# Hybrid decoder step: adaLN shifts taken out of PSUM by ScalarE, S5 tables a unit sooner, one Toeplitz tile for four quarters

## The chip, the cores and the metric

One Trainium2 chip, one NeuronCore of it. The metric is device time in microseconds of one execution; the median of three runs of the kernel before is 1148.75 us.

## The reference

One layer of a decoder works on 1024 prompt positions and 8 single-token sequences with a state of their own. An adaLN vector, `mod = silu(c) @ ada_w + ada_b`, gives shift, scale and gate for two blocks. The first block is what the change touches:

```python
hn = rmsnorm(x, norm1_g) * (1.0 + sc1) + sh1
proj = hn @ w_in                        # 1024 x 1536: RG-LRU input, its gate, S5 input u
# RG-LRU half: causal conv of width 4, gates, real recurrence, times gelu(gate)
# S5 half: 32 groups of 16 channels, each one complex diagonal state of 64
h[t] = a * h[t-1] + B u[t]              # complex, zero-order hold
y[t] = Re(C h[t]) + d * u[t];  z = gelu(y) @ w_glu;  out = za * sigmoid(zb)
```

Both halves are normalised and go through `w_out`, are gated and added to `x`; then come a SwiGLU feed-forward block and a final norm. Outputs are all tokens and the new states.

## The kernel before, in words

Activations lie as feature x token, 1032 tokens wide. Matmuls run with each float32 operand split into a high and a low part, three matmuls for one product (L142 to L144, the helper `mm3`); the split's low part is a VectorE subtraction and appears as `wl_...`.

The stage around the change is the input projection. Its twelve 128-column blocks of `w_in`, in three pieces of 344 tokens, make 36 pieces; the first six are computed in an opening. The other 30 are called units here and stand in the list `SEQ` (L1062), each of 8 x 3 matmuls into one PSUM bank. The rest of the stage is hung in front of units by `at(i, function)` (L1059). What is hung there is the remaining adaLN work (`rest_load`, `rest_dot`, `rest_out`) and the S5 half, in four quarters of eight groups each. A quarter `f_` starts at unit `STARTS[f_]`, that is 5, 9, 14 or 19, and takes these steps at offsets from it (L1055):

- `s5_in_tables`: from the load `bc` the scaled input matrices `bb` (VectorE), their copy `bst` (ScalarE), and the products `pb` (GpSimd, in quarter 0 VectorE).
- `s5_out_tables`: output products `cw` on VectorE, and `ost` from them by ScalarE in two pairs, one for the real and one for the imaginary half.
- `s5_turn`: TensorE transposes `pb` into `ppt`, ScalarE copies to `pst`.
- `s5_toeplitz`: TensorE multiplies `bst` by `ost` into `kp`, ScalarE copies it to `kt`, two VectorE rows add `d`; `kt` goes to DRAM as `kd` (four transfers), and eight transfers read it back as the Toeplitz tile `tm`, which GpSimd has filled with zero.
- `s5_drive` in two halves: TensorE forms `pv` from `u` and `pst`, ScalarE copies to `vt`. Behind the second half comes `s5_state` on VectorE: rotation `rw`, scan, rotation back `dw`; ScalarE copies it to `xt`.
- `s5_out` in two halves: TensorE adds `tm` times `u` and `ost` times `xt` into `py`, ScalarE applies GeLU.

`kp`, `pv`, `ppt`, `py` and the adaLN sums (`pmod`) share two PSUM tiles in turn, so each must wait until the reader of the one before last is done. That reader is VectorE's `mod` row (L69) behind a `pmod`, and ScalarE's `pst`, `vt`, `kt` rows behind others.

`ada_out` (L241) turns a finished adaLN product into `mod`, or, for part 0, into the shifts `shf`; the helper `ada_sum` (L236) does the matmul (`pmod`) and one VectorE row adds the bias `ada_b`. The shifts are then split into the last ten columns of `hnh` and `hnl` (L726) and multiplied with the first two blocks of `w_in` (`bias_dot`, L1064: `pa_b`; `adas_b` is its copy out of PSUM).

TensorE's order is the program's own in the whole kernel. In the opening this also holds for the other engines. In the stage of the 30 units, ScalarE, VectorE, GpSimd and the SyncE queue of transfers take an order that a scheduler made when the program was built. Each engine then runs its list in that order.

Of the kernel before, what the change touches and what calls it, by code (L numbers as in the profile page):

```python
# [9 lines left out]
F32 = mybir.dt.float32  # L10
F32R = mybir.dt.float32r
I32 = mybir.dt.int32
AF = mybir.ActivationFunctionType
# [5 lines left out]
P = 128  # L19
# [35 lines left out]
def body(ctx, tc, a, o):  # L55
    nc = tc.nc
    V, S, G, PE = nc.vector, nc.scalar, nc.gpsimd, nc.tensor
# [10 lines left out]
    def tt(out, x, y, op, e=None):  # L68
        (e or V).tensor_tensor(out=out, in0=x, in1=y, op=op)  # L69
# [16 lines left out]
    def stt(out, x, s, op0, y, op1):  # L86
        V.scalar_tensor_tensor(out=out, in0=x, scalar=s, in1=y, op0=op0, op1=op1)  # L87
# [4 lines left out]
    def small(name):  # L92
        return psm.tile([P, 512], F32, tag="sm", name=name)
# [23 lines left out]
    def par(name):  # L117
        s, w = PACK_AT[name]
        return pk[:, s:s + w]
# [84 lines left out]
    mod = cp.tile([P, 4, DK, 9], F32, name="mod")  # L204
    shf = cp.tile([P, DK, 32], F32, name="shf")
    G.memset(shf, 0.0)
    adab = par("ada_b").rearrange("p (a d) -> p a d", a=6)
# [28 lines left out]
    def ada_sum(sb, pt, n=9, step=16):  # L236
        for i in range(2):
            PE.matmul(pt[:, i * step:i * step + n], lhsT=sb[:, i * P:(i + 1) * P], rhs=sel[:, 0:n], start=True,
                      stop=True)

    def ada_out(sb, pt, part, h):  # L241

        ada_sum(sb, pt, 32, 32)
        d = slice(4 * h, 4 * h + 4)
        dst = mod[:, part - 2, d] if part else shf[:, d, 0:9]
        tt(dst.rearrange("p (q c) n -> p q c n", q=2),
           pt[:, 0:64].rearrange("p (c q n) -> p q c n", c=2, q=2)[:, :, :, 0:9],
           adab[:, part, d].rearrange("p (q c) -> p q c", q=2).unsqueeze(3).to_broadcast([P, 2, 2, 9]), ALU.add)
# [248 lines left out]
    bias = cp.tile([P, 12, 9], F32, name="bias")  # L497
# [157 lines left out]
    for i in range(1, 4):  # L655
        d = 2 * i
# [44 lines left out]
    rsb[1] = ada_second(sh_raw[1], "h1", sb)  # L701
    rstd_spread(r1, "n1", rb1, lambda i: small if i == 2 else lambda n: acc_bank(n, 512))
    ada_out(*rsb[1], 0, 0)
    rsb[2] = ada_dot(sh_raw[2], "h2", small, last=False)
    for c in range(NC):
# [51 lines left out]
    sp2 = []  # L757
    sq = [{} for _ in range(4)]
# [106 lines left out]
    def s5_toeplitz(f_):  # L865

        bst, ost = sq[f_]["bst"], sq[f_]["ost"]
        kp = small(f"kp{f_}")
        for g in range(8):
            st = g % 4  # L870
            PE.matmul(kp[32 * st:32 * st + 32, (g // 4) * P:(g // 4 + 1) * P], lhsT=bst[:, g], rhs=ost[:, g, 0:128],
                      start=True, stop=True, tile_position=(0, 32 * st))
        kt = sp2[0].tile([P, 2, P], F32, tag="kt", bufs=1, name=f"kt{f_}")
        S.activation(kt.rearrange("p a k -> p (a k)"), kp[:, 0:2 * P], AF.Copy)
        for i in range(2):
            stt(kt[:, i, 0:16], sel[:, 0:16], par("dk")[:, 2 * f_ + i:2 * f_ + i + 1], ALU.mult, kt[:, i, 0:16], ALU.add)
        kd = dr.tile([2, 4, 16, P], F32, name=f"kd{f_}")
        for st in range(4):
            nc.sync.dma_start(out=kd[:, st].rearrange("a c k -> c a k"), in_=kt[32 * st:32 * st + 16])
        tm = sp2[0].tile([P, 8, P], F32, tag="tm", bufs=1, name=f"tm{f_}")  # L880
        G.memset(tm, 0.0)
        for j in range(8):
            nc.sync.dma_start(out=tm[16 * j:16 * j + 16, :, 16 * j:],
                              in_=kd.rearrange("a s c k -> c (a s) k")[:, :, 0:P - 16 * j])
        sq[f_]["tm"] = tm
# [158 lines left out]
    def rest_out(j):  # L1044
        p, i = rest[j]
        if j % 2:
            ada_out(rsb[j][0], PB(f"pmod{j}"), p, i // 2)
            if p == 0:
                shift_cols(i - 1)
                shift_cols(i)  # L1050
# [1 line left out]

    R0, R1 = 4, 1.12
    STARTS = (5, 9, 14, 19)
    IT, OT, RT, TZ, DA, DB, OA, TN, OB = 5, 0, 1, 2, 1, 2, 3, 1, 2  # L1055
    CLOSE = 27
    before, mids = {}, {}

    def at(i, fn, *args):  # L1059
        before.setdefault(i, []).append((fn, args))  # L1060
# [19 lines left out]
    for j in range(4, 20):  # L1080
        i = int(R0 + R1 * (j - 4))
# [4 lines left out]
    for f_ in range(4):  # L1086
        i0 = STARTS[f_]
        at(max(0, i0 - IT), s5_in_tables, f_)
        at(max(0, i0 - OT), s5_out_tables, f_)
        at(max(0, i0 - RT), s5_rot, f_)  # L1090
        at(i0 if f_ == 0 else i0 - TN, s5_turn, f_)
        at(i0 + TZ, s5_toeplitz, f_)
        at(i0 + DA, s5_drive, f_, 0)
        at(i0 + DB, s5_drive, f_, 1)
        at(i0 + DB + OA, s5_out, f_, 0)
        at(i0 + DB + OA + OB, s5_out, f_, 1)
# [696 lines left out]
    for mp in range(4):  # L1793
        pool, tag = (hp, "H") if mp < 2 else (fp, "F")
# [157 lines left out]
```

## Time and profile before

| | us |
|---|---|
| runs of the kernel before | 1144.76, 1148.75, 1149.11 |
| the profiled execution | 1144.03, its span 1142.2 |
| TensorE matmul busy | 1086.4 (95%) |
| VectorE busy | 812.9 (71%) |
| ScalarE busy | 518.9 (45%) |
| GpSimd busy | 446.1 (39%) |
| granted TensorE clock, mean | 0.974 of full speed |

The profile is of one execution, and its instructions have start and duration. Busy times are averages over the whole span; between 50 and 250 us TensorE is less busy than later, and VectorE more than its average. The number in brackets behind a row is the time that its engine sat idle before it and what ended this; a wait for several things is put down to the one that came last. A group of equal rows is merged into one with a count, and the trace counts each float32 matmul of a small tile twice.

### The profile page before, as it was taken

The numbers are of one execution on the slowest core, as the hardware profiler recorded it, in microseconds if no ns is written. First come the engines' busy times: TensorE is split into PE (matmuls) and PEld (weight loads), VectorE is DVE, ScalarE is ACT, GpSimd is POOL, SyncE is SP. The second block draws the span as 40 slices with busy tenths as digits, with TensorE's granted clock in tenths as the row PEclk, the third lists the DMA queues.
The fourth block names the chain that finished last, engine by engine and source line by source line (L and its number), as shares of the span: only waits on it lengthen the run. The fifth ranks groups of instructions, "written<-read, shape, count | busy, mean of one in ns | idle before, by whom it ended". The sixth has DMA issues, their size and how long they took to land.

```text
span 1142.2 us, 21509 instructions
## 1 busy us (share of the span) xinstructions
PE 1086.4 (95%) x8508; PEld 1037.0 (91%) x8508; DVE 812.9 (71%) x1335; ACT 518.9 (45%) x979; POOL 446.1 (39%) x478
## 2 busy tenths in 40 slices
PE   8988979998898999899999999999999999999996
PEld 5877868897878999799999999999999999999995
DVE  6596899735966288887587577768645367778967
ACT  4544544439573066555455444545444522122254
POOL 2754665101100014675475466557342133242003
PEclk8989989999998999899999999999999999999998
DMA  9566446341143303153453245334313967468303
GB/s 336 216 188 219 156 146 217 85 130 37 40 148 111 112 38 112 37 205 118 143 186 148 85 177 186 109 131 180 120 56 102 358 264 283 166 238 275 115 8 142
DMA packets 90629, 174.94 MB, mean 153 GB/s; under 512 B 18720, under 2 KB 54304, under 8 KB 90528
## 3 DMA queue, kind: packets, MB, share of 16 engines
q1 hardware_dynamic: 90528, 173.57, 44.1%
q8 instruction: 67, 1.10, 0.4%
q14 instruction: 34, 0.28, 0.1%
HBM read 126.56 MB, written 46.98 MB: 152 GB/s over the span
## 4 chain that ended last, share of the span: by engine, by line
PE 79%; DVE 12%; ACT 3%; issue 3%; DMA 2%; SPq 1%; DVEq 0%; ACTq 0%
PE X L1539 10%; PE X L1540 10%; PE X L1541 10%; PE Y L1540 5%; PE Y L1539 5%; PE Y L1541 5%; PE Z L1539 2%; PE Z L1541 2%; PE Z L1540 2%; PE o L1335 2%; PE o L1334 2%; PE o L1336 2%; PE in L142 2%; PE in L143 2%; PE in L144 2%
## 5 line engine op out<-in xcount | busy, mean ns | idle before, releaser
L69 POOL TENSOR_TENSOR u<-u,p 128x258 f32<-128x258 f32 x44 | 41.8, 949 | 125.7 <-ACT u L1591 125.7
L142 PE MATMUL in<-hnh,wh_in 128*128 128x344 f32 (+1 forms) x240 | 81.3, 339 | 0.0
L143 PE MATMUL in<-hnl,wh_in 128*128 128x344 f32 (+1 forms) x240 | 78.8, 328 | 0.0
L144 PE MATMUL in<-hnh,wl_in 128*128 128x344 f32 (+1 forms) x240 | 78.7, 328 | 0.0
L69 POOL TENSOR_TENSOR st_d<-wf_d 128x256 f32<-128x256 f32 x32 | 26.6, 853 | 110.6 <-PE X L1541 37.0
L69 POOL TENSOR_TENSOR sa_g<-wf_g 128x512 f32<-128x512 f32 x11 | 14.7, 1340 | 134.1 <-PE o L1336 102.9
L69 DVE TENSOR_TENSOR acc<-X,acc 128x258 f32<-128x258 f32 x128 | 49.9, 419 | 10.3 <-PE X L1541 10.1
L142 PEld LDWEIGHTS in<-hnh,wh_in 128*128 128x128 f32 x240 | 46.8, 195 | 2.9 <-issue 2.9
L1591 ACT ACTIVATE u<-X 128x258 f32<-128x258 f32 x88 | 33.2, 381 | 31.8 <-PE X L1541 31.5
L143 PEld LDWEIGHTS in<-hnl,wh_in 128*128 128x128 f32 x240 | 46.8, 195 | 0.0
L69 DVE TENSOR_TENSOR hs<-v,hs 128x516 fp32r<-128x516 f32 x32 | 46.1, 1456 | 0.9 <-ACT hs L1409 0.9
L144 PEld LDWEIGHTS in<-hnh,wl_in 128*128 128x128 f32 x240 | 46.5, 194 | 0.0
L1335 PE MATMUL o<-ls,wh_s 128*128 128x258 f32 x128 | 38.4, 300 | 4.3 <-DVE ls L69 4.3
L1336 PE MATMUL o<-hs,wl_s 128*128 128x258 f32 x128 | 37.8, 296 | 0.0
L1334 PE MATMUL o<-hs,wh_s 128*128 128x258 f32 x128 | 37.8, 295 | 0.0
L87 DVE SCALAR_TENSOR_TENSOR xz<-o,mod,xz 128x258 f32<-128x258 f32 (+1 forms) x32 | 15.4, 480 | 30.5 <-PE o L1336 27.9
L1334 PE MATMUL o<-hl,wh_l 128*128 128x258 f32 x128 | 36.8, 287 | 0.1
L1335 PE MATMUL o<-ll,wh_l 128*128 128x258 f32 x128 | 36.3, 284 | 0.3 <-DVE ll L69 0.3
L1336 PE MATMUL o<-hl,wl_l 128*128 128x258 f32 x128 | 36.2, 283 | 0.0
L69 POOL TENSOR_TENSOR acc<-acc,rbf 128x388 f32<-128x388 f32 x10 | 11.7, 1203 | 60.8 <-ACT rbf L201 60.8
L69 POOL TENSOR_TENSOR v<-u 128x516 f32<-128x516 f32 x16 | 21.3, 1332 | 32.7 <-DVE u L69 32.7
L69 DVE TENSOR_TENSOR acc<-Y,acc 128x258 f32<-128x258 f32 x64 | 26.5, 423 | 9.9 <-PE Y L1541 9.4
(1652 smaller groups left out, 4798.4 us busy)
## 6 DMA issues: line engine op xcount, KB each, us to landing
ht<-hs SPq DMA_DIRECT2D x48, 516.0 KB, 3.0
db<-ht SPq DMA_DIRECT2D x48, 516.0 KB, 8.2
ad<-ada SPq DMA_DIRECT2D x48, 512.0 KB, 6.3
wf_g<-w_gu SPq DMA_DIRECT2D x22, 512.0 KB, 4.0
wf_u<-w_gu SPq DMA_DIRECT2D x22, 512.0 KB, 3.4
wf_d<-w_dn SPq DMA_DIRECT2D x16, 512.0 KB, 3.9
wf_in<-w_in SPq DMA_DIRECT2D x10, 512.0 KB, 4.7
x<-xt SPq DMA_DIRECT2D x8, 516.0 KB, 8.2
```

The lines of the kernel that those rows point to most:

```text
L69: (e or V).tensor_tensor(out=out, in0=x, in1=y, op=op)
L87: V.scalar_tensor_tensor(out=out, in0=x, scalar=s, in1=y, op0=op0, op1=op1)
L142: PE.matmul(ps, lhsT=wh, rhs=xh, start=first, stop=False)
L143: PE.matmul(ps, lhsT=wh, rhs=xl, start=False, stop=False)
L144: PE.matmul(ps, lhsT=wl, rhs=xh, start=False, stop=last)
L1334: PE.matmul(b, lhsT=wh, rhs=xh, start=half == 0 and k == 0, stop=False)
L1335: PE.matmul(b, lhsT=wh, rhs=xl, start=False, stop=False)
L1336: PE.matmul(b, lhsT=wl, rhs=xh, start=False, stop=half == 1 and k == 3)
L1539: PE.matmul(b, lhsT=wh, rhs=xh, start=first and k == 0, stop=False, skip_group_check=True)
L1540: PE.matmul(b, lhsT=wh, rhs=xl, start=False, stop=False, skip_group_check=True)
L1541: PE.matmul(b, lhsT=wl, rhs=xh, start=False, stop=k == nk - 1, skip_group_check=True)
L1591: S.activation(k[name], b[bank], AF.Copy)
```

## The change

Three parts. First, in `ada_out` the shifts leave PSUM by four ScalarE rows with `ada_b` as their bias in place of one VectorE row. Second, two offsets change: `s5_out_tables` is hung one unit earlier (OT from 0 to 1) and `s5_toeplitz` too (TZ from 2 to 1). Third, `s5_toeplitz` ends with the store of `kd`; a new function loads `tm`, hung at the later of that unit and the unit of the previous quarter's last `s5_out`. The tile is allocated and filled with zero in quarter 0 alone and serves all four, since each load writes the same block triangle.

```diff
@@ ada_out
-        dst = mod[:, part - 2, d] if part else shf[:, d, 0:9]
+        if not part:
+            for i in range(4):
+                S.activation(shf[:, 4 * h + i, 0:9], pt[:, 32 * (i % 2) + 16 * (i // 2):32 * (i % 2) + 16 * (i // 2) + 9],
+                             AF.Identity, bias=adab[:, 0, 4 * h + i:4 * h + i + 1])
+            return
+        dst = mod[:, part - 2, d]
@@ s5_toeplitz
-        tm = sp2[0].tile([P, 8, P], F32, tag="tm", bufs=1, name=f"tm{f_}")
-        G.memset(tm, 0.0)
+        sq[f_]["kd"] = kd
+
+    def s5_toeplitz_load(f_):
+        kd = sq[f_]["kd"]
+        if f_ == 0:
+            sq[0]["tm"] = sp2[0].tile([P, 8, P], F32, tag="tm", bufs=1, name="tm")
+            G.memset(sq[0]["tm"], 0.0)
+        tm = sq[0]["tm"]
         for j in range(8):
             nc.sync.dma_start(out=tm[16 * j:16 * j + 16, :, 16 * j:],
                               in_=kd.rearrange("a s c k -> c (a s) k")[:, :, 0:P - 16 * j])
@@ offsets
-    IT, OT, RT, TZ, DA, DB, OA, TN, OB = 5, 0, 1, 2, 1, 2, 3, 1, 2
+    IT, OT, RT, TZ, DA, DB, OA, TN, OB = 5, 1, 1, 1, 1, 2, 3, 1, 2
@@ the loop over the quarters
         at(i0 + TZ, s5_toeplitz, f_)
+        at(max(i0 + TZ, STARTS[f_ - 1] + DB + OA + OB if f_ else 0), s5_toeplitz_load, f_)
```

Line numbers of the new kernel are 5 higher behind the first part and 11 higher behind the new function. On TensorE only the four groups of `kp` move, each a unit earlier. The scheduler gives the other engines new orders; three places follow.

ScalarE at units 1 and 2, around the copy `adas_b`. Before (L729 is the shift's high part, L734 the bias of `up`):

```order
L230 ACTIVATE adas_r_3_881<-pa_h_792 128x256
L729 ACTIVATE hnh_464<-shf 128x10
L729 ACTIVATE hnh_471<-shf 128x10
L729 ACTIVATE hnh_566<-shf 128x10
L729 ACTIVATE hnh_573<-shf 128x10
L800 ACTIVATE bst_840<-bb_839 64x4x16 x2
L230 ACTIVATE adas_b<-pa_b 128x256
L800 ACTIVATE bst_840<-bb_839 64x4x16 x2
L734 ACTIVATE up_683<-up_683,bias 128x1024
```

The same place now:

```order
L230 ACTIVATE adas_r_3_884<-pa_h_795 128x256
L247 ACTIVATE shf<-pmod_893,pk 128x9 x4
L734 ACTIVATE hnh_464<-shf 128x10
L734 ACTIVATE hnh_471<-shf 128x10
L734 ACTIVATE hnh_566<-shf 128x10
L734 ACTIVATE hnh_573<-shf 128x10
L805 ACTIVATE bst_843<-bb_842 64x4x16 x4
L230 ACTIVATE adas_b<-pa_b 128x256
L739 ACTIVATE up_683<-up_683,bias 128x1024
```

The four shift rows have come in, and `adas_b` stands behind all four `bst` rows instead of between the pairs. On VectorE, `bb`, from which the second pair of `bst` is made, has moved ahead of one `up` row. In front of it `wl_in` of two weights stands as before.

ScalarE at units 6 and 7, the copies of quarter 0's `pv` with the tables of quarter 1. Before:

```order
L914 ACTIVATE vt_1198<-pv_0_1199 64x136 x4
L914 ACTIVATE vt_1198<-pv_1_1206 64x136 x4
L230 ACTIVATE adas_r_1_1256<-pa_r_0_1185 128x256
L874 ACTIVATE kt_1271<-kp_1262 128x256
L800 ACTIVATE bst_1045<-bb_1044 64x4x16 x4
L914 ACTIVATE vt_1198<-pv_2_1290 64x136 x4
L914 ACTIVATE vt_1198<-pv_3_1297 64x136 x4
```

The same place now:

```order
L879 ACTIVATE kt_1213<-kp_1204 128x256
L925 ACTIVATE vt_1232<-pv_0_1233 64x136 x4
L925 ACTIVATE vt_1232<-pv_1_1240 64x136 x4
L805 ACTIVATE bst_1065<-bb_1064 64x4x16 x4
L230 ACTIVATE adas_r_1_1290<-pa_r_0_1191 128x256
L925 ACTIVATE vt_1232<-pv_2_1296 64x136 x4
L925 ACTIVATE vt_1232<-pv_3_1303 64x136 x4
```

`kt` has moved to the front, and `bst` ahead of `adas_r`. On GpSimd the fill of that `bst` has moved from behind the last products of quarter 1 to a place two products earlier.

TensorE at unit 10, where quarter 0's output meets quarter 1's drive. Before:

```order
L963 MATMUL py_3_1560<-u_950,tm_1280 128x136
L965 MATMUL py_3_1560<-xt_1322,ost_1110 128x136
L910 MATMUL pv_0_1567<-u_962,pst_1392 128x136 x2
L910 MATMUL pv_1_1574<-u_962,pst_1392 128x136 x2
```

The same place now:

```order
L974 MATMUL py_3_1566<-u_956,tm 128x136
L976 MATMUL py_3_1566<-xt_1328,ost_1039 128x136
L876 MATMUL kp_1572<-ost_1389,bst_1065 32x128 x8
L921 MATMUL pv_0_1591<-u_968,pst_1412 128x136 x2
L921 MATMUL pv_1_1598<-u_968,pst_1412 128x136 x2
```

`kp` of quarter 1, which stood a unit later behind an adaLN product, now comes between `py` and `pv`. VectorE's order from there to quarter 1's last `cw` row is as before. In quarter 2 ScalarE's `lx` goes ahead of three `vt` rows; in quarter 3 VectorE's `mod` goes behind two more `cw` rows.

## Rows read from the trace of the kernel before

**Rows 1.** What TensorE waited for, whole span: us in total, times, longest.

```profile
PE py L963 <- DVE mod L69: 6.3, 3, 3.2
...
PE pmod L238 <- ACT pst L861: 3.9, 2, 2.7
PE ppt L858 <- DVE mod L69: 3.7, 1, 3.7
PE pa_b L225 <- DVE shf L69: 3.6, 1, 3.6
```

**Rows 2.** Windows of 50 us: length, busy us (instructions), PEclk, DMA share, GB/s.

```profile
100.00:150.00 50.00, 41.56 (x332) 36.36 (x332) 43.97 (x73) 22.85 (x51) 25.49 (x27) 0.97 0.49 151
```

**Rows 3.** Timelines of PE, ACT, DVE, 65 to 71: start, us, idle before.

```profile
67.13 1.08 PE L225 MATMUL pa_b<-w_raw,shf 128*32 128x256 f32 x8 [3.60 <-DVE shf L69]
69.27 1.03 PE L238 MATMUL pa_b<-ct,adas_b 128*128 128x9 f32 x4
...
68.86 0.36 ACT L230 ACTIVATE adas_b<-pa_b 128x256 f32<-128x256 f32 x1
70.12 0.52 ACT L800 ACTIVATE bst<-bb 64x64 f32<-64x64 f32 x2 [0.90 <-DVE bb L69]
...
65.17 1.21 DVE L69 TENSOR_TENSOR wl_in<-wf_in,wh_in 128x1024 fp32r<-128x1024 f32 x1
...
68.36 0.75 DVE L69 TENSOR_TENSOR up<-in,rb 128x344 f32<-128x344 f32 x1
...
69.75 0.30 DVE L69 TENSOR_TENSOR bb<-bb,bw 128x64 f32<-128x64 f32 x1
```

**Rows 4.** Windows of 4 us: PE, PEld, DVE, ACT, POOL busy, then PEclk.

```profile
68.00:72.00 4.00, 4.00 (x17) 3.52 (x14) 3.97 (x13) 2.44 (x6) 2.99 (x12) 0.50 0.84 247
72.00:76.00 4.00, 4.00 (x23) 4.00 (x23) 3.02 (x11) 1.15 (x1) 3.17 (x6) 0.86 0.51 137
...
108.00:112.00 4.00, 4.00 (x18) 3.82 (x17) 3.12 (x6) 1.27 (x3) 1.45 (x2) 0.66 0.97 341
120.00:124.00 4.00, 1.47 (x13) 1.32 (x12) 4.00 (x8) 1.46 (x3) 2.07 (x3) 1.00 0.97 313
```

**Rows 5.** Timelines of ACT, DVE, PE, 97 to 113: quarter 0's state.

```profile
97.91 1.06 ACT L800 ACTIVATE bst<-bb 64x64 f32<-64x64 f32 x4 [2.50 <-POOL bst L789]
...
101.04 2.01 DVE L69 TENSOR_TENSOR rw<-et,vt 128x512 f32<-128x512 f32 x3 [4.78 <-ACT vt L914]
...
112.15 0.52 DVE L69 TENSOR_TENSOR lx<-in,rb 128x344 f32<-128x344 f32 x1 [0.96 <-PE in L144]
...
106.10 0.66 PE L858 MATMUL ppt<-ident,pb 128*128 128x128 f32 x4 [3.70 <-DVE mod L69]
```

**Rows 6.** Timelines of DVE, ACT, PE, 122 to 128: unit 10.

```profile
122.44 0.18 DVE L69 TENSOR_TENSOR mod<-pmod,pk 128x36 f32<-128x36 f32 x1
...
123.87 0.75 DVE L69 TENSOR_TENSOR cw<-cw,cw 128x576 f32<-128x576 f32 x1
...
125.61 1.40 ACT L833 ACTIVATE ost<-cw 64x576 f32<-64x576 f32 x2
...
123.71 1.38 PE L910 MATMUL pv<-u,pst 128*128 128x136 f32 x8
```

**Rows 7.** Timelines of DVE, ACT, PE: quarter 1's state, quarter 3's tables.

```profile
133.67 3.88 DVE L69 TENSOR_TENSOR rw<-et,vt 128x512 f32<-128x512 f32 x3 [1.23 <-POOL pw L69]
...
203.63 1.38 ACT L833 ACTIVATE ost<-cw 64x576 f32<-64x576 f32 x2 [3.71 <-DVE cw L69]
...
202.37 1.19 PE L910 MATMUL pv<-u,pst 128*128 128x136 f32 x8
```

**Rows 8.** Timelines of DVE and POOL: scans of two quarters, the fill.

```profile
104.60 1.36 DVE L934 TENSOR_TENSOR_SCAN vt<-mag,rw 128x128 f32<-128x128 f32 x4
...
140.64 1.36 DVE L934 TENSOR_TENSOR_SCAN vt<-mag,rw 128x128 f32<-128x128 f32 x4
...
141.51 0.95 POOL L881 MEMSET tm<- 128x1024 f32 x1 [0.30 <-issue]
```

## Prediction

> **What bounds the kernel now.** First the list of what TensorE (PE) waited for, then windows with each engine's busy time and the granted clock, then the timelines of PE, ScalarE (ACT) and VectorE (DVE) around each wait. All that the diff touches lies between 55 and 230 us of the span. Four of the five costliest waits of the list are in it [rows 1]: `py` for DVE's `mod` 6.3 us, `pmod` for ACT's `pst` 3.9, `ppt` for `mod` 3.7, the second half of `pa_b` for `shf` 3.6; together 17.5 us, and this is what the change can hope for. A second price hangs on them. After the 3.60 us wait the granted clock stands at 0.50, the lower of PE's two levels (1.2 instead of 2.4 GHz), until about 73.1 (0.86 over the four us from 72 is 1.1 us at that level); after the 3.70 us wait it is 0.66 over 108 to 112, which is 2.7 us at the lower level or 1.4 us of lost work. The gap of 2.53 us in 120 to 124 (busy 1.47 of 4.00) left the clock at 1.00 [rows 3 to 5]. What PE waits for is an instruction deep in another engine's line: DVE is busy 43.97 of the 50 us from 100 [rows 2]. So the reader has to see what stands ahead of the awaited row, on its own engine, after the change. No wait of PE on a `tm` load is among them: to issue these loads by themselves removes none of them.
>
> **The change part by part.** Times are those of the profiled execution; "late" and "early" compare with it.
>
> A. Shifts by ACT. On ACT four ACTIVATEs of 128 x 9 come right behind `adas_r`. No row shows this form; from below it costs nothing, from above four times `adas_b` (128 x 256 out of PSUM, 0.36), 1.4. PE needs the result at 63.5 (67.13 less 3.60), some 3 us behind `pmod`, so either way the wait goes. Next PE is stopped by `wl_in` of the next weight, which DVE ends at 66.4 [rows 3]: PE gets there at 64.9 (1.08 of `pa_b` and two matmuls later) and waits 1.5. Then comes `pa_b` out of `adas_b`, before at 69.27. There ACT ran `adas_b` at 68.86 between two pairs of `bst` rows; now all four stand ahead of it, and the second pair needs DVE's last `bb`. This ended at 70.05; in the new order the `up` row (0.75, of which 0.1 overlaps) goes behind it: 69.4. The pair (0.52) ends at 69.9, `adas_b` at 70.3. PE goes on at 70.3 and not at 69.27: 1.0 late, where the wait alone says 3.6 early.
> The Trainium skill (TensorE: Matmul & The Clock Gate, "Architectural detail") says that ScalarE and VectorE take their queues strictly first in, first out. By it `adas_b` cannot pass the pair; could it pass, PE would go on at 66.5, 2.8 early, and the sum would be 3.8 lower. The trace agrees as far as it goes: ACT sat idle 0.90 us before the pair.
> Clock: before, 69.27 to 73.1 at the lower level cost 1.9 us. Now PE idles 1.5 and 3.8 us with three matmuls between. Before, the lower level ended 6.0 us after PE had resumed at 67.13; I take the same 6.0 us from 70.3, which costs 3.0, so 1.1 more. If it ends at 73.1 all the same it costs 1.4, or 0.5 less than before. A gives +2.1, bounds +0.5 and +2.1.
>
> B. `kp` a unit sooner, quarter 0. ACT's `bst` of quarter 1 stood idle 2.50 us for GpSimd's fill of its tile and held up `vt` until 98.97 (97.91 + 1.06); the fill now goes ahead of two GpSimd products. ACT was free at 95.4 (97.91 less 2.50); plus PE's 2.1 that is 97.5, plus an estimated 0.3 until `pv` is out, 97.8: `vt`, and behind it DVE's `rw` (101.04), are 1.2 early. From `rw` to `mod` DVE's rows are the same in number, so `mod` and with it `ppt` come at 104.9 for 106.10 [rows 5]. PE, 2.1 late, is there at 104.5 (106.10 less 3.70, plus 2.1): it waits 0.4 and not 3.7, and I drop the 1.4 us of lower clock. PE leaves this unit 2.6 early. DVE's 0.96 us of idle before `lx` at 112.15 closes with PE's lead: DVE is 2.15 early.
>
> C. `kp` a unit sooner, quarter 1. DVE's order is unchanged: `mod` (122.44), `xc`, then the last `cw` add (123.87 + 0.75). `mod` is now at 120.3, `py` behind it at 120.5 (PE is ready at 117.5, 122.62 less 2.53 less 2.6: a gap of 2.9). Where PE went straight on to `pv` at 123.71 now stands `kp`, which reads both halves of `ost`. The second half needs that add: 124.62 less 2.15 is 122.5, plus the pair's 1.40 is 123.9 [rows 6]. PE waits again, 2.4 us, and has at 123.9 what it had at 123.71: 0.2 late, the whole lead of B is gone. For two gaps of 2.9 and 2.4 I charge 1.4 us of lower clock (bounds 0 and 1.9, the two prices seen): 1.6 late. The time of `kp` itself is only moved.
>
> D. The rest of quarters 1 to 3, where DVE sets the pace. On ACT `kt` (a copy like `adas_b`, 0.36) no longer stands before the second `vt`, so `rw` at 133.67 is 1.3 late. Three `rw` took 3.88 us there beside GpSimd's products, against 2.01 with GpSimd idle [rows 5, 7]. These products now start earlier relative to `rw`, and I credit one such difference, 1.9; bounds 0 and three times 1.9, one for each quarter. Quarter 1 ends 0.6 early. In quarter 2 `lx` on ACT comes before three `vt` rows (0.26 each, from `bst`): 1.4 early. Against it, `mod` of quarter 3's unit stands behind two more `cw` rows (0.7 each): 0.0. Last, `kp` of quarter 3 needs `ost`, ready at 203.63 + 1.38 = 205.0, where PE began `pv` at 202.37: a new wait of 2.6, less the 1.4 by which `cw` is early: 1.2 late [rows 7].
> Three fills of `tm` go (0.95 each). I take 0 for them: the fill at 141.51 ran beside DVE's scans, which took 1.36 as in quarter 0 [rows 8]. The Trainium skill (GPSIMD Engine Reference, 1. Specifications) says that GpSimd shares its SBUF interfaces with VectorE and that DVE instructions with two SBUF inputs contend; by it up to 2.85 us of DVE's time would come back and the sum would be that much lower. The row does not show it for this fill.
> The SyncE queue holds the same transfers as before, `tm` again behind the `py` of the quarter before.
>
> Sum: A +2.1, B -4.7 (to 2.6 early), C +4.2 (to 1.6 late), D -0.4 (to 1.2 late). After 230 us PE's order is as before, so 1.2 stays: 1144.0 + 1.2 = 1145.2 for the profiled execution. The median of the runs lies 4.7 above that execution; on its scale this is 1149.9. The bounds: A 1.6, C 1.4 and D 3.8 lower; C 0.5 and D 1.9 higher.
>
> **The rivals.** *No change* (mine): each wait removed hands PE to the next row of the same DVE line: 1149.9, its own range 1144 to 1153.
>
> *Faster*: DVE's line shortens. GpSimd's work moves away from `rw` in all three quarters (a further 3.8), `ost` of quarter 3 then comes before PE needs it (1.2), and the clock stays up in A and C (1.1 and 1.4): 7.5 less, 1142. For it: DVE lost 1.9 in one group of rows 7. Against it: GpSimd's products of quarters 2 and 3 keep their places, and DVE's rows are as many as before but for two.
>
> *Slower*: `kp` waits for `ost`, where nothing was late before. The second half of `ost` falls due a unit sooner with its products still at the old place on DVE. The price is 126.0 less 123.71, 2.3 in quarter 1, and 2.6 in quarter 3, with 1.4 of clock each; less 0.4 and 0.8 on ACT, and without D's credit, that is +6.5: 1155. It decides once DVE has gained nothing at B, that is if the fill of `bst` still comes after `pv`; A's 2.1 then vanishes in the wait for `mod`. For it: rows 6 and 7 show both dates. Against it: the cause of the 2.50 us of idle in rows 5 has moved.
>
> **How the numbers follow.** 0.5% (5.7 us) is about what a measurement of this kernel can tell from no change. No change 0.64, faster 0.19, slower 0.17. The likeliest gives the time. The range starts at 1140, since the runs before reach 4 us below their median and most of the faster case lies above that, and ends at 1155.
>
> **What would show it.** In the new trace no wait of `pa_b` on `shf`; instead `in` for DVE's `wl_in` 1.5 and `pa_b` for ACT's `adas_b` 3.8; `ppt` for `mod` under 1; `kp` for ACT's `ost` some 2.4 in quarter 1 and up to 2.6 in quarter 3; `py` for `mod` still 2 to 4 each time. I am wrong if `adas_b` runs before 69, if `kp` never waits, or if PE's waits before 230 us sum to less than 12.

## The result and the profile after

| | before | after |
|---|---|---|
| median of 7 runs, us | 1147.01 (1144.62 to 1149.11) | 1153.46 (1152.11 to 1155.71) |
| the profiled execution | 1144.03, span 1142.2 | 1153.01, span 1151.2 |
| TensorE matmul busy | 1086.4 | 1085.3 |
| granted TensorE clock, mean | 0.974 | 0.976 |

The changed kernel takes 1.0054 times as long, 95% interval 1.0035 to 1.0072: slower, and clear of no change; the half per cent that the prediction took for the smallest difference lies inside the interval. The two profiled executions lie 9.0 us apart and the medians 6.4, since the profiled execution of before is a quick one among its own runs (1143.9 to 1154.5 over all the comparisons below). The two traces also differ by 0.9 us before anything that the change touches: the copy `adas_h` in the opening runs at 54.41 before and at 53.48 after. Against that mark, every number of the column "late" below is 0.9 higher.

What TensorE waited for after the change (us in total, times, longest), beside [rows 1]:

```profile
PE py L974 <- DVE mod L69: 11.3, 3, 3.9
PE pv L921 <- ACT kt L879: 5.4, 2, 4.4
...
PE pa_b L238 <- ACT adas_b L230: 2.7, 1, 2.7
...
PE pmod L238 <- ACT pst L866: 1.2, 2, 1.0
PE kp L876 <- ACT ost L838: 1.2, 1, 1.2
PE ppt L863 <- DVE mod L69: 1.1, 1, 1.1
```

The waits for `shf` (3.6), `pst` (3.9) and `ppt`'s for `mod` (3.7) have gone or shrunk, as the change meant. Three have come: `pv` for `kt`, which the prediction does not name, `kp` for `ost`, and one of 0.96 us of `py` for the transfers of `tm` in quarter 1 (157.21), which a longer wait for `mod` right behind it (3.83) took up. `py`'s waits for `mod` have grown from 6.3 to 11.3. Where the time went, place by place (TensorE begins this row; minus is early):

| place | before | after | late |
|---|---|---|---|
| quarter 0's `ppt` | 82.58 | 80.23 | -2.4 |
| adaLN product of unit 7 | 93.45 | 97.62 | +4.2 |
| adaLN product behind quarter 1's `ppt` | 112.04 | 111.00 | -1.0 |
| adaLN product of unit 11 | 128.79 | 135.01 | +6.2 |
| second `py` of quarter 1 | 158.75 | 162.67 | +3.9 |
| second `py` of quarter 2 | 196.45 | 204.07 | +7.6 |
| last `pmod` | 220.82 | 230.05 | +9.2 |

Behind 230 us the two are alike. So there are three bad stretches (units 6, 10 and the end of quarter 2); behind the first two some of the loss is recovered. The stretches one by one.

Timelines of TensorE and ScalarE of the changed kernel, 84 to 92:

```profile
85.98 0.62 PE L876 MATMUL kp<-ost,bst 128*32 128x128 f32 x16
86.53 0.73 PE L921 MATMUL pv<-u,pst 128*128 128x136 f32 x4
91.61 0.60 PE L921 MATMUL pv<-u,pst 128*128 128x136 f32 x1 [4.36 <-ACT kt L879]
...
85.03 1.06 ACT L96 ACTIVATE wh_in<-wf_in 128x1024 fp32r<-128x1024 f32 x1 [2.95 <-PE in L143]
90.14 1.15 ACT L739 ACTIVATE up<-up,bias 128x1024 f32<-128x1024 f32 x1 [4.05 <-DMA ad<-ada]
91.20 0.36 ACT L879 ACTIVATE kt<-kp 128x256 f32<-128x256 f32 x1
```

and of VectorE there:

```profile
87.49 0.23 DVE L69 TENSOR_TENSOR bb<-fr,bc 128x64 f32<-128x64 f32 x1 [5.26 <-DMA bc<-s5bc]
...
88.41 0.98 DVE L69 TENSOR_TENSOR bb<-bb,bw 128x64 f32<-128x64 f32 x1
89.32 0.73 DVE L69 TENSOR_TENSOR up<-in,rb 128x336 f32<-128x336 f32 x2
89.96 0.15 DVE L82 TENSOR_SCALAR bias<-in 128x9 f32<-128x9 f32 x1
```

Read it from the end. The second `pv` needs the PSUM tile that `kp` holds, because the two small tiles go round in turn; `kt` is the copy that sets it free. `kt` is ready to run at 86.6 and runs at 91.20, since `up` stands ahead of it on ScalarE; `up` needs VectorE's `bias` (90.1), and that stands behind the six `bb` and `bw` rows of quarter 1, which wait for the transfer `bc` until 87.49. (The releaser printed at `up`, an adaLN transfer, is only the last semaphore event; `bias` at 89.96 plus 0.15 fits to 0.03.) Before, the same `up` ran at 89.89 and delayed only `vt`, for which TensorE did not wait there:

```profile
89.89 1.16 ACT L734 ACTIVATE up<-up,bias 128x1024 f32<-128x1024 f32 x1 [1.45 <-DVE bias L82]
```

The lead of 2.4 us is lost here, and 3.1 us run at the lower clock behind it.

TensorE's timeline of the changed kernel, 122 to 131, then its windows of 4 us (as [rows 4]); before, the clock stayed at 1.00 in all four:

```profile
123.05 0.82 PE L974 MATMUL py<-u,tm 128*128 128x136 f32 x2 [3.93 <-DVE mod L69]
...
126.42 1.78 PE L876 MATMUL kp<-ost,bst 128*32 128x128 f32 x16 [1.19 <-ACT ost L838]
128.13 2.18 PE L921 MATMUL pv<-u,pst 128*128 128x136 f32 x8
```

```profile
120.00:124.00 4.00, 0.95 (x4) 0.95 (x5) 4.00 (x6) 1.74 (x2) 2.08 (x2) 0.76 0.98 292
124.00:128.00 4.00, 2.74 (x22) 1.67 (x21) 3.65 (x7) 1.76 (x3) 0.97 (x2) 0.50 0.83 307
128.00:132.00 4.00, 4.00 (x18) 3.87 (x16) 1.15 (x7) 2.76 (x10) 1.41 (x2) 0.50 0.09 22
132.00:136.00 4.00, 4.00 (x35) 3.21 (x33) 0.65 (x2) 0.57 (x3) 0.16 (x1) 0.96 0.02 4
```

The group of eight `pv` takes 2.18 us here and 1.19 at 98.62: TensorE runs at 1.2 GHz. (`kp`'s 1.78 us hold a wait besides: it needs the second pair of `ost`, which ends at 127.08.) Half of the busy time at the lower level is lost work: 0.5 + 1.4 + 2.0 + 0.2, some 4 us, behind two gaps of 3.93 and 1.19.

Not all of this is due to `kp`. The trace of before is the exception here. In shift_only below, where `kp` is at its old place, a wait of 2.60 at the same `py` was enough for the lower level. Windows of before, then two of shift_only:

```profile
124.00:128.00 4.00, 3.98 (x27) 3.77 (x27) 3.28 (x5) 3.73 (x11) 0.67 (x1) 1.00 0.70 269
...
120.00:124.00 4.00, 1.61 (x8) 1.61 (x9) 4.00 (x8) 1.08 (x2) 2.07 (x3) 0.84 0.94 289
124.00:128.00 4.00, 4.00 (x23) 4.00 (x22) 2.99 (x5) 3.04 (x8) 0.38 (x1) 0.73 0.65 253
```

That is 3.4 us at the lower level, 1.7 of lost work, and shift_only begins unit 11's product at 129.87, where the changed kernel has 135.01.

VectorE's and TensorE's timelines at the end of quarter 2; `mod` of this place was at 196.21 before, 7.6 sooner. First the line of before, then the changed kernel:

```profile
196.21 0.18 DVE L69 TENSOR_TENSOR mod<-pmod,pk 128x36 f32<-128x36 f32 x1
...
201.43 0.75 DVE L69 TENSOR_TENSOR cw<-apw,bc 128x576 f32<-128x576 f32 x1
202.09 1.81 DVE L69 TENSOR_TENSOR cw<-cw,cw 128x576 f32<-128x576 f32 x1
203.83 0.18 DVE L69 TENSOR_TENSOR mod<-pmod,pk 128x36 f32<-128x36 f32 x1
...
204.07 0.82 PE L974 MATMUL py<-u,tm 128*128 128x136 f32 x2 [3.56 <-DVE mod L69]
```

Two `cw` rows (2.40 us from start to `mod`) have come ahead of `mod`, and VectorE's whole line is late by then.

### The profile page after: what moved, and what is told of

The parts are those of the page before. It is cut to its first block, busy times and chain, and to the rows that moved or that the text cites. A ratio compares the mean times of both kernels' runs of the same rounds, so it can differ in the third digit from the quotient of the medians.

```text
span 1151.2 us, 21502 instructions
## 1 busy us (share of the span) xinstructions
PE 1085.3 (94%) x8508; PEld 1035.9 (90%) x8508; DVE 813.7 (71%) x1333; ACT 520.4 (45%) x987; POOL 448.0 (39%) x475
## 4 chain that ended last, share of the span: by engine, by line
PE 78%; DVE 12%; ACT 4%; issue 3%; DMA 2%; POOL 1%; SPq 0%; DVEq 0%; ACTq 0%; POOLq 0%
PE X L1551 10%; PE X L1552 9%; PE X L1553 9%; PE Y L1551 5%; PE Y L1553 5%; PE Y L1552 5%; PE in L142 2%; PE Z L1553 2%; PE Z L1552 2%; PE Z L1551 2%; PE o L1347 2%; PE in L143 2%; PE o L1348 2%; PE o L1346 2%; PE in L144 2%
```

## The experiments

Ratios are to the kernel before, from five rounds each; a thousandth is 1.15 us.

| run | what it has of the change | besides | ratio | interval |
|---|---|---|---|---|
| (the change) | all | | 1.0054 | 1.0035 to 1.0072 |
| shift_only | shifts | | 0.9987 | 0.9968 to 1.0006 |
| kp_late | shifts, one tile, own loads | | 1.0053 | 1.0035 to 1.0072 |
| kp_late_own | shifts, own loads | | 0.9996 | 0.9981 to 1.0012 |
| own_tile | all but the one tile | | 1.0046 | 1.0028 to 1.0063 |
| kp_bank | all | `kp` in a unit's bank | 1.0014 | 0.9997 to 1.0031 |
| fill_q1 | all | idle matmuls in two gaps | 1.0030 | 1.0014 to 1.0045 |
| bank_fill_q1 | all | both of these | 0.9981 | 0.9964 to 0.9997 |
| after_bst | all | one `bst` tile | 1.0053 | 1.0034 to 1.0073 |
| bst_only | nothing | one `bst` tile | 0.9987 | 0.9970 to 1.0004 |
| shift_bst | shifts | one `bst` tile | 0.9939 | 0.9916 to 0.9961 |
| kp_late_bst | shifts, one tile, own loads | one `bst` tile | 0.9950 | 0.9933 to 0.9968 |

The offset `OT` has no part in it: with it back at 0 every engine's list of instructions is the same, row for row.

**shift_only**: the diff's first part alone, on the kernel before.

> The kernel before with the first part of the change alone: the shifts by ScalarE, everything else as before. Theory (a wait removed here is only handed on): as in the profile after, TensorE leaves the wait for adas_b 2.1 us sooner and begins the unit-6 adaLN product near 85.1 instead of 87.44; but quarter 0's mod still hangs on vt behind the bst rows, which wait for GpSimd, so ppt waits about 6 us instead of 3.7 and nothing is left: 1147, ratio 0.998 to 1.002. Rival (the lead survives): all later steps come 2.35 us sooner, 1144.7, ratio 0.998 or less. Second rival (the new VectorE order that the scheduler makes is what costs): 1150 or more, ratio above 1.003.

1147.24, ratio 0.9987. The interval holds the rival's bound of 0.998 too; the trace decides for the first theory. The lead was there (unit-6 product at 85.36; 0.8 of the 2.1 was there from the opening on), and ScalarE's `bst` waited it away:

```profile
97.64 1.06 ACT L805 ACTIVATE bst<-bb 64x64 f32<-64x64 f32 x4 [3.80 <-POOL bst L794]
98.70 2.33 ACT L919 ACTIVATE vt<-pv 64x136 f32<-64x136 f32 x8
```

against an idle time of 2.50 and a `bst` at 97.91 before [rows 5]. `ppt` went on at 105.83 instead of 106.10. One point was missed: its wait stayed 3.70, since `pmod` in front of it already waited 1.49 for `vt`.

**kp_late**: `TZ` back to 2 in the changed kernel.

```diff
-    IT, OT, RT, TZ, DA, DB, OA, TN, OB = 5, 1, 1, 1, 1, 2, 3, 1, 2
+    IT, OT, RT, TZ, DA, DB, OA, TN, OB = 5, 1, 1, 2, 1, 2, 3, 1, 2
```

> The changed kernel with kp back at its old unit (TZ = 2); the shifts by ScalarE and the single Toeplitz tile with its separate loads stay. Theory (kp a unit sooner is the whole loss): no wait of pv for kt, no wait of kp for ost, and no long stretch at the lower clock behind unit 10; the time falls back to that of the kernel before, 1145 to 1148, ratio 0.997 to 1.002. Rival (the single tile, its load order or the new VectorE order has a share in the loss): 1149 to 1152, ratio 1.002 to 1.004.

1152.99, ratio 1.0053: my theory fell, and the rival's side is met, above its range. With `kp` at its old place the kernel is as slow as with `kp` sooner. Up to 175 us it runs with shift_only (0.4 behind); then, ScalarE of kp_late:

```profile
175.62 0.86 ACT L925 ACTIVATE vt<-pv 64x136 f32<-64x136 f32 x3 [0.34 <-PE pv L921]
179.58 1.05 ACT L805 ACTIVATE bst<-bb 64x64 f32<-64x64 f32 x4 [3.10 <-POOL bst L794]
180.65 1.47 ACT L925 ACTIVATE vt<-pv 64x136 f32<-64x136 f32 x5
```

and of shift_only:

```profile
175.18 2.34 ACT L919 ACTIVATE vt<-pv 64x136 f32<-64x136 f32 x8 [0.34 <-PE pv L915]
179.38 1.05 ACT L805 ACTIVATE bst<-bb 64x64 f32<-64x64 f32 x4 [1.86 <-POOL bst L794]
```

GpSimd's fill lets `bst` go at the same time in both. But in the order that the scheduler made without `tm`'s fills, `bst` stands ahead of five `vt` rows. These end at 182.1 and not 177.5; VectorE's first `rw` is at 181.84 and not 179.19, and `py` of quarter 2 goes on at 201.11 and not 197.65.

**kp_late_own**: kp_late with a tile and a fill for each quarter again.

```diff
-        if f_ == 0:
-            sq[0]["tm"] = sp2[0].tile([P, 8, P], F32, tag="tm", bufs=1, name="tm")
-            G.memset(sq[0]["tm"], 0.0)
-        tm = sq[0]["tm"]
+        tm = sp2[0].tile([P, 8, P], F32, tag="tm", bufs=1, name=f"tm{f_}")
+        G.memset(tm, 0.0)
```

> The changed kernel with kp at its old unit (TZ = 2) and with a Toeplitz tile of its own and its fill in each quarter: of the change there remain the shifts by ScalarE and the loads issued by themselves. Theory (with kp at its old unit, taking away the fills lets the scheduler put bst of quarter 3 ahead of quarter 2's vt, where it waits for GpSimd, and two cw rows ahead of mod; that is the loss of 5.8 us against the shifts alone): vt is whole by 177.6 again instead of 182.1, py of quarter 2 goes on near 197.7 instead of 201.1, and the time is that of the shifts alone, 1146 to 1148, ratio 0.997 to 1.001. Rival (the loads issued by themselves cost, through SyncE's order of transfers): 1151 to 1153, ratio 1.003 or more.

1148.0, ratio 0.9996. Three fills put back, and the kernel is 0.0057 faster: `vt` is whole at 177.3, `mod` of quarter 2 comes at 196.71 instead of 200.88, and `py` does not wait for it. (In this trace the adaLN product in front waited 1.9 us for its transfer, which the loads' new order on SyncE may have brought; in the total it does not show.)

**own_tile**: the same edit in the changed kernel, with `kp` sooner.

> The changed kernel with a Toeplitz tile of its own, filled with zero by GpSimd, in each quarter as before; kp stays a unit sooner and the loads stay by themselves. The orders of TensorE, VectorE and ScalarE are those of the changed kernel row for row; GpSimd has three fills of 0.95 us more. Theory (three fills are worth nothing, as predicted; the cost of the single tile seen with kp at its old unit is one of order alone): 1152 to 1155, the same as the changed kernel, ratio 1.004 to 1.007. Rival (the fills hold up VectorE's products, as one share of SBUF would have it): up to 2.85 us slower than the changed kernel, ratio 1.007 or more.

1154.14, ratio 1.0046, within the interval of the change. With `kp` sooner the fill of `bst` comes early anyway, the order of TensorE, VectorE and ScalarE is the same with and without the fills, and the fills are worth nothing. So `kp` sooner and the one tile each cost 0.005 to 0.006 where the other is not there, and together they cost no more: `kp` sooner heals what the one tile spoils, and brings a loss of its own of the same size.

**kp_bank**: `kp` out of the two small tiles.

```diff
-        kp = small(f"kp{f_}")
+        kp = acc_bank(f"kp{f_}", 512)
```

> The changed kernel with kp in a PSUM bank out of the five that the units use in turn, instead of one of the two small tiles; pv then no longer waits for kt, the copy of kp. Nothing else changes but a few places in the order. Theory A (that stall of 4.36 us and the 1.5 us of lower clock behind it cost the end): vt of quarter 0 and with it rw and mod come about 3.7 us sooner, ppt goes on near 103 instead of 106.65, and all that follows is 3.7 sooner; in quarter 2 another 1.06: 1149, ratio 1.001 to 1.003. Rival B (the stall was taken up at once by the wait for mod, since TensorE was 1.0 us ahead of the kernel before at 111; the loss is made in quarters 1 and 3): 1153, ratio 1.005, with ppt again near 106.5 after a longer wait.

1148.78, ratio 1.0014: theory A. `pv` goes without that stop though `kt` is no sooner (91.52), and what hangs on it is 3.5 us earlier (`rw`, and `ppt` at 103.11 for 106.65). TensorE and VectorE of kp_bank, where the changed kernel has 91.61 for the second `pv` and 101.46 for `rw`:

```profile
86.87 1.19 PE L921 MATMUL pv<-u,pst 128*128 128x136 f32 x8
...
97.92 1.90 DVE L69 TENSOR_TENSOR rw<-et,vt 128x512 f32<-128x512 f32 x3 [4.40 <-ACT vt L925]
```

**fill_q1**: TensorE kept at work in the two gaps of unit 10.

```diff
+    def fill(n, name):
+        b = acc_bank(f"fill{name}")
+        for _ in range(n):
+            PE.matmul(b[:, 0:P], lhsT=ident, rhs=ident, start=True, stop=True)
...
+        if f_ == 1:
+            fill(9, "kp")
         kp = small(f"kp{f_}")
...
+            if f_ == 0 and g0 == 3:
+                fill(16, "py")
             py = small(f"py{f_}_{g0}")
```

> The changed kernel with matmuls of the identity into an unused bank, 16 before the second half of quarter 0's first output (py, which waits 3.93 us for mod) and 9 before quarter 1's kp (which waits for ost): TensorE works through both gaps. No result uses them. Theory A (the lower clock from 123.0 to about 132.4, some 4.7 us of lost work, is the largest term of the loss): the clock stays at its upper level, kp still begins near 126.4 but pv, and the next unit with it, end 3 us sooner: 1150 to 1151, ratio 1.003. Rival B (behind unit 10 VectorE sets the pace, so TensorE's clock there costs nothing in the end): 1153, ratio 1.005.

1149.65, ratio 1.0030, the time of theory A. Windows of fill_q1 (the same stretch as above, the kernel being 0.7 late at its start):

```profile
120.00:124.00 4.00, 3.63 (x32) 3.44 (x32) 4.00 (x7) 2.38 (x3) 2.00 (x3) 1.00 0.98 298
124.00:128.00 4.00, 4.00 (x44) 3.53 (x44) 4.00 (x6) 1.94 (x4) 1.79 (x3) 1.00 0.96 369
128.00:132.00 4.00, 4.00 (x29) 3.97 (x28) 2.45 (x10) 3.46 (x13) 2.33 (x4) 1.00 0.10 25
```

`py` and `kp` begin when they did (123.71, 126.84), but at 2.4 GHz, and unit 11's product comes at 132.70 and not 135.01. The intervals of fill_q1 and of the change overlap by a thousandth, so the gain is shown, but its size only roughly.

**bank_fill_q1**: both edits, with 10 and 8 idle matmuls.

> The whole change with kp in a PSUM bank of the five that the units use (as in kp_bank) and with matmuls of the identity ahead of quarter 0's second py (10) and of quarter 1's kp (8), as in fill_q1. Nothing uses their result. Theory (kp a unit sooner costs by two separate things, pv's wait for kt in quarter 0 and the long stretch at the lower clock in quarter 1; alone, their removal gave 0.0040 and 0.0024): both together give 0.0064, so 1146 to 1147, ratio 0.998 to 1.000. Rival (they remove the same loss, since both end in a wait for mod): 1148 to 1149, ratio 1.001 to 1.002.

1146.85, ratio 0.9981. The single gains (0.0040 and 0.0024) add to 0.0064; measured 0.0073. They are two losses, not one seen twice, and with both gone the time of the shifts alone (0.9987) is reached again; the interval ends at 0.9997. The idle matmuls, though, also take away the lower clock that shift_only has at this place. So this does not show that nothing else of `kp`'s loss is left: the end of quarter 2 still waits 5.30 us for `mod`. Idle matmuls in a kernel with `kp` at its old place were not run.

**shift_bst**: the shifts, and a `bst` tile that is filled once. The copies into it move behind `kp` of the quarter before, which reads the tile.

```diff
-        bst = sp.tile([P, 8, 32], F32, tag="bst", bufs=1, name=f"bst{f_}")
-        G.memset(bst, 0.0)
+    def s5_bst(f_):
+        if f_ == 0:
+            sq[0]["bst"] = sp.tile([P, 8, 32], F32, tag="bst", bufs=1, name="bst")
+            G.memset(sq[0]["bst"], 0.0)
...
+    at(0, s5_bst, 0)
+    for f_ in range(1, 4):
+        at(STARTS[f_ - 1] + TZ, s5_bst, f_)
```

> The kernel before with the shifts by ScalarE, and with one bst tile for all quarters: GpSimd fills it once, and a quarter's copies into it stand behind kp of the quarter before. Kp stays at its old unit, the Toeplitz part is as before. Theory (what holds quarter 0's vt back is GpSimd's fill of bst, which stands at the end of its line though it could run at once): ScalarE no longer idles 2.5 us before bst; quarter 0's first rw comes near 98.5 instead of 101, ppt goes on near 103.4 instead of 105.8 and the granted clock stays up behind it; the rest comes 2 to 3.5 us sooner: 1143.5 to 1145, ratio 0.996 to 0.9985. Rival (vt early only lengthens the next wait for mod, VectorE's line sets the end of quarters 1 to 3): 1147, ratio 0.998 to 1.001.

1142.03, ratio 0.9939, the best of all, faster than both kernels and by more than I expected. ScalarE of shift_bst; against shift_only the second `vt` group is 4.8 us sooner, 1.4 of which the whole trace is early:

```profile
92.55 0.24 ACT L821 ACTIVATE bst<-bb 64x64 f32<-64x64 f32 x1
92.69 0.36 ACT L884 ACTIVATE kt<-kp 128x256 f32<-128x256 f32 x1
93.08 0.79 ACT L821 ACTIVATE bst<-bb 64x64 f32<-64x64 f32 x3
93.88 2.34 ACT L924 ACTIVATE vt<-pv 64x136 f32<-64x136 f32 x8
```

`rw` comes at 95.95, `ppt` goes on at 101.33 after 1.76 of waiting, the last `pmod` at 219.61. The edit changes two things, the number of fills and the place of the copies; no run separates them.

**bst_only**: the same without the shifts.

> The kernel before with only the single bst tile of the run shift_bst: one fill by GpSimd, a quarter's copies behind kp of the quarter before; the shifts stay with VectorE. Theory (the shifts by ScalarE are worth 1.1 to 1.5 us, as they showed alone; the rest of shift_bst's gain is the fill's): ScalarE does not idle before bst, the first rw comes near 98 instead of 101.04, ppt goes on near 103.3 instead of 106.1; 1143 to 1145, ratio 0.995 to 0.997. Rival (the lead from the shifts is needed for the gain: without it TensorE's own pv, at 94.9, comes too late): ratio 0.998 or more.

1147.3, ratio 0.9987: the times in the trace are those of the theory (`rw` 98.60, `ppt` 103.79), the total is the rival's. ScalarE runs `vt` at 96.53, 2.65 later than in shift_bst, since `pv` itself comes at 95.07; 1.2 of this the whole trace is late. Of the lead of 3.9 us over before at 108, 2.5 is left when `mod` comes (119.94), and the clock takes the rest:

```profile
120.18 0.82 PE L968 MATMUL py<-u,tm 128*128 128x136 f32 x2 [3.92 <-DVE mod L69]
```

Behind this wait the clock is at its lower level, where the trace of before kept the upper one, and unit 11's product is at 128.67 against 128.79. In shift_bst the wait is 2.56; the clock falls there too, but the product comes at 125.36. Each edit alone gives 0.0013, which its interval does not tell from nothing, and both 0.0061. That `vt` needs `pv` as well as ScalarE's place, so that one of them late is enough, fits this; no run shows it by itself.

**after_bst** and **kp_late_bst**: the same tile in the changed kernel, and in kp_late.

> The whole change with the single bst tile besides. With kp a unit sooner the fill of bst comes early as it is. Theory (what is left of the loss is kp's own place: pv waits for kt, kp for ost): no gain from this edit, 1151 to 1154, ratio 1.003 to 1.006. Rival (the fill is the one cause of all losses): ratio 0.999 or less.

> The run kp_late (the change with kp at its old unit), with the single bst tile of the run shift_bst besides. Theory (the 5.8 us that kp_late lost against the shifts alone were ScalarE's wait for the fill of bst ahead of vt, and the mod behind it): with the fill gone the loss is gone too, and quarter 0's gain comes on top as in shift_bst: 1141 to 1144, ratio 0.993 to 0.997. Rival (the loss came from VectorE's order, with two cw rows ahead of quarter 2's mod, or from the one Toeplitz tile itself): ratio 0.999 or more.

1154.07, ratio 1.0053, and 1144.79, ratio 0.9950: the theory both times by the ratio. A `bst` that is filled in each quarter is what kp_late lost by, and no part of what `kp` sooner loses by.

## Why the prediction was right or wrong, point by point

The time lay within the range (1140 to 1155), 1.5 us from its upper end, but the likeliest case, no change at 1149.9, did not come. The slower one did, by about its own time: it says +6.5, measured is +6.4. This is luck. Its terms were `kp`'s waits for `ost` in quarters 1 and 3 with their clock; the second did not occur, and in its stead stands a wait that no rival had, `pv` for `kt`.

- **A**: wrong in sign. The step that failed is "`bb` ended at 70.05; in the new order 69.4". In the changed kernel that row ends at 66.14, `adas_b` runs at 66.72, TensorE goes on at 67.15 (+1.0 forecast, 2.1 early measured, 0.9 of it from the opening), and there is no wait for `wl_in`. VectorE, ScalarE, TensorE of the changed kernel:

```profile
65.93 0.21 DVE L69 TENSOR_TENSOR bb<-bb,bw 128x64 f32<-128x64 f32 x1
...
66.72 0.38 ACT L230 ACTIVATE adas_b<-pa_b 128x256 f32<-128x256 f32 x1
...
67.15 0.75 PE L238 MATMUL pa_b<-ct,adas_b 128*128 128x9 f32 x4 [2.73 <-ACT adas_b L230]
```

  I had kept VectorE's old times and moved single rows in them; its `bb`, `pb` and `wl_in` rows here ran 3.3 to 3.9 us sooner. Three things are in this: the 0.9 from the opening; the opening's own shift row, which the edit also takes from VectorE's line, where it came at 56.75 behind 3.13 us of idle time, with the four `up` rows behind it (55.01 now, 56.87 before); and three rows `bb`, `bw`, `bb` that take 0.7 together and took 2.7 (last section). The clock was better too: the lower level ended 3.8 us after TensorE went on (the windows read 0.50 from 68 to 70, 0.55 from 70 to 71, and 1.00 behind it), not 6.0. That `adas_b` keeps its place behind the four `bst` was right. On its own the part gains little (shift_only), for the reason forecast for the whole: the lead meets the next wait.
- **B**: `bst` early, right (94.21, no wait); `ppt` for `mod` "0.4 and not 3.7" was 1.10, and the low clock behind it went. The step that failed is "`vt`, and behind it `rw`, are 1.2 early": `rw` came at 101.46 and not 99.85. `kp` sooner puts a third user of the two PSUM tiles into unit 6, and I did not ask who frees its tile, though the order rows had `kt` at the front of ScalarE's list. kp_bank prices this at 0.0040, 4.6 us.
- **C**: the gap before `py` was 3.93 (2.9 forecast), `kp`'s wait for `ost` 1.19 (2.4). The mechanism was right and together they fit; the size that was off is the clock, 1.4 charged, about 4.0 measured and 2.8 given back by fill_q1. My bound of 1.9 came from single gaps [rows 4], and 1.7 is lost here in shift_only as well.
- **D**: "`mod` behind two more `cw` rows (0.7 each)" happened, with 2.40 for 1.4; `kp` of quarter 3 did not wait for `ost` at all (2.6 forecast), since TensorE was later than `ost` by then. Of the 1.9 credited for `rw` beside GpSimd's products 0.9 came (2.99 for 3.88). "Three fills: 0" holds with `kp` sooner (own_tile) and is wrong with `kp` late, by 0.0057, through the order: work was taken away, and the time rose. The loads by themselves cost nothing that the total shows (kp_late_own against shift_only), as said, though they did not come without a new wait for `tm`.
- **The signs named**: `pa_b` for `shf` gone, `py` for `mod` 3.93, 3.83 and 3.56 ("2 to 4") came as said, `ppt` 1.10 ("under 1") nearly so; `pa_b` for `adas_b` was 2.73 and not 3.8. "I am wrong if `adas_b` runs before 69" is met, at 66.72. TensorE's waits of the list between 55 and 230 sum to 26.0, not under 12, and were 19.0 before: waits moved and did not go, which is what "no change" rested on.
- **The slower rival** was to decide "once DVE has gained nothing at B", and VectorE had gained nothing at B (101.46 against 101.04); but by PSUM, not by the fill coming late, and quarter 3's half of its price did not occur.
- **The range of "no change"**: its own bounds give 1143 to 1152 (6.8 down, 2.4 up), where "1144 to 1153" is written. The scale was off as well: with seven runs the median of before is 1147.01, 3.0 above the profiled execution and not 4.7.

## What to carry to other kernels

When an instruction moves that takes a rotating buffer, list who frees each buffer in turn, and what stands ahead of that copy on its engine: here a copy of 0.36 us stopped TensorE for 4.4. With a scheduler, an edit that only takes work away can cost through the new order, so build the edit both with and without that work before crediting it. And before moving a consumer away from a late producer, ask why the producer is late: filling `bst` once gave 0.5% beside the shifts, and moving `kp` cost as much.

## What the runs showed of the hardware

- VectorE's small rows can last as long as a GpSimd product beside them. VectorE before, 62 to 66:

```profile
62.67 1.24 DVE L69 TENSOR_TENSOR bb<-fr,bc 128x64 f32<-128x64 f32 x1
63.83 0.21 DVE L69 TENSOR_TENSOR bw<-fi,bc 128x64 f32<-128x64 f32 x1
63.97 1.28 DVE L69 TENSOR_TENSOR bb<-fr,bc 128x64 f32<-128x64 f32 x1
```

and GpSimd there:

```profile
62.78 1.05 POOL L69 TENSOR_TENSOR ew<-eta,etb 128x512 f32<-128x512 f32 x1
63.91 1.26 POOL L69 TENSOR_TENSOR et<-et,ew 128x512 f32<-128x512 f32 x1
```

  Both `bb` rows end within 0.1 us of a GpSimd product's end; the same row took 0.23 at 87.49 in the changed kernel, with GpSimd idle. The Trainium skill (GPSIMD Engine Reference, 1. Specifications) says that the two share SBUF interfaces and that VectorE's instructions with two SBUF inputs contend. The trace agrees, by a factor of 5 for so short a row. It is part of why A's VectorE line ran sooner than I had it; no run here separates that part.
- One gap does not always have one price in clock. At quarter 0's second `py`, a wait of 2.53 left the clock at 1.00 from 120 to 128 in the trace of before; waits of 2.60 in shift_only, 2.57 in kp_late, 2.56 in shift_bst and 2.52 in kp_bank were all followed by the lower level. This may be one reason why runs of the kernel before spread over 10 us. It is in any case why 0.2% is not seen in two profiles: the trace of before begins the last `pmod` 2.8 us ahead of shift_only's (220.82, 223.61), and their medians do not differ so.
